# Gate tiles kept to their plan from both sides, and the first two gate tiles of a layer computed side by side

## The chip, the core and the metric

The kernel runs on one core of one Trainium2 chip. What counts is the device time of one launch in microseconds, the median of the runs. The core's engines run their own instruction streams and meet only through semaphores: TensorE (PE: matrix products and transposes; PEld is its weight load), VectorE (DVE), ScalarE (ACT), GpSimd (POOL), and SyncE (SP), which issues the transfers.

## The reference

A backbone of two layers over 512 latent tokens and 256 context tokens, width 1024, all in float32. A layer makes six modulation vectors out of a conditioning vector, modulates and normalizes its input, runs four kinds of attention over one large projection, weighs each attention's projected output with a gate, and ends with a feed-forward block.

```python
mod = (jax.nn.silu(c) @ lp['w_mod'] + lp['b_mod']).reshape(B, 1, N_MOD, D_MODEL)
h = modulate(x, mod[:, :, 0], mod[:, :, 1])            # the same for the context: mod_c, hc
aq, ak, av, bq, bkv, cq, ck, cv, dq, dk, dv, g = split_columns(h @ lp['w_in'])
oa, ob, oc, od = ...                                   # diff, MLA, grid and window attention
y = jnp.einsum('btke,ked->btkd', jnp.stack(outs, axis=2), w_branch)
gate = jax.nn.sigmoid(g.reshape(B, T, N_BRANCH, D_MODEL))
out = jnp.sum(gate * y, axis=2) @ w_out                # merge_branches
x = x + mod[:, :, 2] * mix
x = x + mod[:, :, 5] * conv_ffn(modulate(x, mod[:, :, 3], mod[:, :, 4]), lp)
```

The gates are 4 x 1024 of the columns of `w_in`: 32 tiles of 128 columns, which need the modulated input alone and are first used when the branches are merged. The modulation vectors 2 to 5 of a layer are also first used behind its attention.

## The kernel before

**Layout.** Activations lie with features on the partitions and the 768 tokens along the free axis (512 latent, 256 context), a width of 1024 as 8 feature tiles. A float32 product is made as three matmuls of split operands: `hh`,`whi`, then `hl`,`whi`, then `hh`,`wlo`. So a projection tile of 128 output columns takes 24 matmuls for each chunk of tokens. A weight tile comes in by DMA (`wraw`), ACT or DVE rounds it to `whi`, and DVE or POOL makes the rest `wlo`. Five such pairs of 128x512 can be held at a time (`WSLOTS`); a gate tile takes two of them.

**What sets the order.** The program's instructions are not emitted in the order of the code. A planner (`Clock`, with `defer` and `flush`) keeps a modelled time for each engine, and each engine's stream is sorted by planned start. What goes to PE next is chosen by `Flow` (L370 to L464) out of generators ("streams") of these kinds:

- `live`: the attention units of the layer, and `aux`: small work that belongs to them;
- `urgent`: the projections that attention is about to need;
- `gates`: the 32 gate tiles of the layer, then the merge and the feed-forward, used as filler wherever attention can't keep PE busy;
- `back`: the modulation vectors of later use.

`head` offers the first urgent or gate stream that is ready. In `run`, a stream of `urgent` is served while `debt` is positive; debt grows as attention steps are served. Otherwise the first ready step of `cand = aux + live + back` is taken, and only if none is ready the filler that `head` offers. `limit()` says how many gate tiles should still be left at this point of the attention, so that they last; `spared` keeps those back. Nothing pulls a gate tile forward that is behind this plan.

**The modulation vectors.** `diff_open` pushes vectors 2, 4, 3 and 5 of layer 0 to `back` while the attention runs: 64 steps, each with a load of 256 KB (`wm`) and two DVE instructions (`macc`, `maccc`, 128x512 each; one step in 8 is on ACT); every 8 steps end with transposes on PE (`tr<-ident,macc`, `tr<-ident,maccc`). `MPACE` is the least distance between two steps, in the planner's microseconds.

**The merge.** `open_merge` (L1538) opens the merge of the branches once nothing is in `urgent` or `gates` and the pool of the diff attention is closed, and that closes only when `back` is empty. It frees the modulated input (`hh`, `hl`) and uses the room for the attention outputs, which come back from DRAM (`oraw`, then split into `oh` and `ol`). `g_merge` multiplies them with `w_branch` (`d<-oh,whi` and so on).

**The gates.** `open_gates` (L803) makes one stream `g_gate` (L810) for each of the 32 tiles. In layer 0 it is called once the input of the layer has been loaded, in layer 1 at the end of layer 0; there the 512 latent tokens alone are computed, as the last layer leaves the context out. A tile is 24 matmuls into one PSUM bank per chunk, then a tanh on ACT (`gt`) and a store. The first tiles of a layer run while its features (`hh`, `hl` of feature tile 0, 1, ...) are still being made, one after the other.

Of the kernel before, what the change touches and what calls it, by code (L numbers as in the profile page):

```python
# [9 lines left out]
P = 128  # L10
NX, NC_, NT = 512, 256, 768
DM = 1024
KD = DM // P
# [22 lines left out]
MPACE = 5.5  # L36
# [190 lines left out]
def _body(tc, io, dump):  # L227
# [144 lines left out]
    class Flow:  # L372
# [5 lines left out]
        def __init__(self):  # L378
            self.aux, self.urgent, self.gates, self.back, self.pumps = [], [], [], [], []
            self.cur = None  # L380
            self.limit = lambda: 0

        def prefetch(self):
            for q in (self.urgent, self.gates):
                for i, s in enumerate(q):
                    if s.started:
                        continue
                    if s.slots > len(wfree):
                        break
                    if self.spared(q, i) and (any(x.started and not x.begun for x in q) or  # L390
                                              len(wfree) - s.slots < RESERVE):
                        break
                    if s.slots == 0:
                        s.started = i == 0
                        break
                    s.step()
                    s.started = True
                    break

# [30 lines left out]
        def run(self, streams, aux_too=False, drain=False):  # L430
            debt = 0.0
            live = [Stream(g) for g in streams]
            while True:
# [10 lines left out]
                if debt > 0 and f and (f is self.cur or f in self.urgent) and f.at() + MARGIN <= t0:  # L444
                    self.fill(f)
                    debt -= clock.pe - t0
                    continue
                cand = self.aux + live + self.back
# [14 lines left out]
                if self.urgent or (self.cur and debt > 0):  # L463
                    debt += PACE * (clock.pe - t0)  # L464
# [338 lines left out]
    def open_gates(l, h, ok, pl):  # L803
        gt_pool[:] = [pl]
        gd[:] = [dr.tile([P, NT], F32, f"gd{l}_{t}") for t in range(32)]
        for t in range(32):
            st = Stream(g_gate(l, t, h, ok, gd[t]), 2)
            st.later = True
            flow.gates.append(st)

    def g_gate(l, t, h, ok, dst):
# [3 lines left out]
        def evac(ps, o, n):  # L815
            g = gt_pool[0].tile([P, NX], F32, "gt", RB["gt"][l])
            nc.scalar.activation(g[:, :n], ps[:, :n], AF.Tanh, scale=0.5)
            nc.sync.dma_start(dst[:, o:o + n], g[:, :n])
# [9 lines left out]
    for l in range(2):  # L828
# [21 lines left out]
        flow.pumps[:] = []  # L850
        aux, urgent, gates = flow.aux, flow.urgent, flow.gates
# [692 lines left out]
        def open_merge():  # L1544
# [6 lines left out]
            flow.pumps.append(load_o)  # L1551
            gates.extend(Stream(g_merge(f, k), 1) for k, f in order)
# [283 lines left out]
        if not last:  # L1836
            xd = [dr.tile([P, NX], F32, f"xd{f}") for f in range(KD)]
            hok = covered(norms)
            flow.limit = lambda: 32 - NGT
# [118 lines left out]
```

## Time and profile before

| | |
|---|---|
| median of 3 runs | 3007.7 us (3001.59 to 3012.05) |
| the profiled execution | 3005.46 us, span 3003.7 us |
| busy: PE / DVE / ACT / POOL | 96% / 67% / 44% / 24% |
| granted PE clock, mean | 0.987 of full speed |
| attention of layer 0, up to its last gate matmul | 293 to 945.2 us |
| rest of it, and the first merge tiles | 945.2 to 1001.1 us |
| start of layer 1 (first gate tile) | 1761.3 us |
| last gate tile and first merge of layer 1 | 2444.2 us |

Times within the profile are microseconds from the start of the span. A matmul's row gives its start, its duration, its engine and line, the tiles it writes and reads, and in brackets the idle time of its engine ahead of it with the instruction that ended this idle time. Durations of neighbouring matmuls overlap; the distance between two starts is what a matmul takes of PE.

### The profile page before, as it was taken

Reading aid. Unit: us, or ns where it says so; the run is one execution under the profiler, and the core shown is the slowest. Engines: PE = TensorE matmul, PEld = TensorE weight load, DVE = VectorE, ACT = ScalarE, POOL = GpSimd, SP = SyncE. Lnnn points to the kernel's source line nnn. Section 1 sums busy time; section 2 is a strip of 40 time slices with the busy share of each in tenths; the row PEclk is TensorE's granted clock in tenths of the full one; section 3 lists DMA queues with packets and bytes.
Section 4 is the critical chain, followed back from the end, with each engine's and each line's share of the span. In section 5 each row is a group of like instructions: output and inputs, shape, how many; then the busy total and the mean of one; then the engine's idle time right before and its main releaser. Section 6 shows DMA issues by size and latency. Waiting matters only on the chain. (4 is left out here: it accounts for less than half of the span.)

```text
span 3003.7 us, 45158 instructions
## 1 busy us (share of the span) xinstructions
PE 2890.9 (96%) x16404; PEld 2476.5 (82%) x16404; DVE 2013.6 (67%) x4004; ACT 1314.2 (44%) x2521; POOL 711.2 (24%) x566
## 2 busy tenths in 40 slices
PE   7999999999997999999999999999999999999998
PEld 4888879888886888888888877788888887888887
DVE  5576777776877666976665475776766777765556
ACT  4465445355554224433333244654445653433333
POOL 2111221212110232322222122122322222332222
PEclk9999999999998999999999999999999999999999
DMA  5332333323223644443332143332222245433333
GB/s 209 102 106 64 116 111 101 116 73 96 96 77 123 201 149 150 129 132 120 113 124 75 55 141 109 102 87 88 92 86 80 90 134 180 148 93 100 95 92 102
DMA packets 183455, 334.58 MB, mean 111 GB/s; under 512 B 22720, under 2 KB 39360, under 8 KB 183232
## 3 DMA queue, kind: packets, MB, share of 16 engines
q1 hardware_dynamic: 183232, 331.70, 35.4%
q8 instruction: 129, 2.11, 0.3%
q14 instruction: 94, 0.77, 0.1%
HBM read 263.97 MB, written 35.65 MB: 100 GB/s over the span
## 5 line engine op out<-in xcount | busy, mean ns | idle before, releaser
L190 POOL TENSOR_TENSOR wlo<-wraw,whi 128x512 fp32r<-128x512 f32 (+1 forms) x407 | 516.2, 1270 | 1876.6 <-ACT whi L190 1230.3
L290 PE MATMUL d<-hh,whi 128*128 128x512 f32 (+1 forms) x1736 | 632.4, 364 | 15.3 <-ACT rt L190 5.4
L290 PE MATMUL d<-hl,whi 128*128 128x512 f32 (+1 forms) x1736 | 615.9, 355 | 1.4 <-DVE hl L190 1.3
L290 PE MATMUL d<-hh,wlo 128*128 128x512 f32 (+1 forms) x1736 | 615.8, 355 | 0.0
L190 ACT CAST whi<-wraw 128x512 fp32r<-128x512 f32 (+1 forms) x537 | 319.1, 597 | 481.6 <-PE d L290 244.7
L290 PEld LDWEIGHTS d<-hh,whi 128*128 128x128 f32 x1736 | 328.8, 189 | 55.0 <-ACT rt L190 6.1
L290 PEld LDWEIGHTS d<-hh,wlo 128*128 128x128 f32 x1736 | 328.2, 189 | 48.7
L290 PEld LDWEIGHTS d<-hl,whi 128*128 128x128 f32 x1736 | 329.0, 190 | 40.6 <-DVE hl L190 3.6
L190 DVE TENSOR_SCALAR_CACHE_REDUCE S<-s 128x512 f32<-128x512 f32 (+2 forms) x576 | 287.0, 515 | 103.0 <-PE s L290 100.3
L190 DVE SCALAR_TENSOR_TENSOR pl<-tr,ph 128x512 fp32r<-128x512 f32 (+2 forms) x364 | 229.5, 650 | 107.4 <-ACT ph L190 105.1
L190 ACT CAST ph<-tr 128x512 fp32r<-128x512 f32 (+2 forms) x364 | 194.8, 558 | 224.5 <-PE tr L295 208.1
L290 PE MATMUL s<-k,qs 128*128 128x256 f32 (+2 forms) x1152 | 279.8, 335 | 7.9 <-DVE qs L190 4.1
L190 ACT ACTIVATE S<-S,stat 128x768 f32<-128x768 f32 (+2 forms) x320 | 257.9, 809 | 45.4 <-DVE stat L190 44.9
L190 DVE SCALAR_TENSOR_TENSOR wlo<-wraw,whi 128x512 fp32r<-128x512 f32 x271 | 197.6, 732 | 112.7 <-ACT whi L190 105.0
L290 PEld LDWEIGHTS s<-k,qs 128*128 128x128 f32 x1152 | 193.0, 189 | 36.4 <-DVE S L190 5.5
L295 PE MATMUL tr<-ident,S 128*128 128x128 f32 x1360 | 197.8, 273 | 3.2 <-DVE S L190 1.3
L295 PEld LDWEIGHTS tr<-ident,S 128*128 128x128 f32 x1360 | 163.6, 140 | 32.6 <-DVE S L190 2.5
L290 PE MATMUL pv<-ph,V 128*128 128x256 f32 (+2 forms) x448 | 165.0, 375 | 2.1 <-ACT ph L190 2.0
L290 PE MATMUL pv<-pl,V 128*128 128x512 f32 (+2 forms) x392 | 144.2, 372 | 8.6 <-DVE pl L190 8.5
L290 PE MATMUL s<-hh,whi 128*128 128x512 f32 (+1 forms) x368 | 131.7, 358 | 0.4 <-ACT hh L190 0.4
L290 PE MATMUL s<-hl,whi 128*128 128x512 f32 (+1 forms) x368 | 131.2, 357 | 0.4 <-DVE hl L190 0.3
L290 PE MATMUL s<-hh,wlo 128*128 128x512 f32 (+1 forms) x368 | 130.7, 355 | 0.0
(277 smaller groups left out, 6047.8 us busy)
## 6 DMA issues: line engine op xcount, KB each, us to landing
wraw<-wp_d SPq DMA_DIRECT2D x220, 256.0 KB, 2.9
wraw<-wup_d SPq DMA_DIRECT2D x176, 256.0 KB, 2.6
wm<-wm_d SPq DMA_DIRECT2D x160, 256.0 KB, 2.9
wraw<-wd_d SPq DMA_DIRECT2D x74, 256.0 KB, 2.7
gd<-gt SPq DMA_DIRECT2D x64, 256.0 KB, 2.0
wraw<-wb_d SPq DMA_DIRECT2D x64, 256.0 KB, 3.5
k<-k SPq DMA_DIRECT2D x80, 192.0 KB, 3.4
wraw<-wo_d SPq DMA_DIRECT2D x56, 256.0 KB, 2.9
```

Of the source, the lines that this page charges most:

```text
L190: self.enter(op, args, kw, lambda: fn(*args, **kw))
L290: clock.defer(t, None, clock.pe - t, names, lambda: real.tensor.matmul(out, lhsT, rhs, start=start, stop=stop))
L295: clock.defer(t, None, clock.pe - t, names, lambda: real.tensor.transpose(out, src, ident[:rows, :rows]))
```

## The change

The diff has five parts. (1) `MPACE` is 7.0 in place of 5.5. (2) A flag `planned` is true from the start of a layer's attention until the merge opens; while it is true the modulation steps stand first among the candidates, ahead of `aux` and the attention, not last. (3) `due()` is true when more gate tiles are left than the plan plus one; then the gate stream is served against `debt` as an urgent one is. (4) The first two gate tiles of a layer become one stream `g_gates2` with four weight slots: for each feature tile the three matmuls of the first gate tile, then the three of the second, into two banks. (5) The limit at the end of layer 0 counts this double stream as one: 31 - (NGT - 1) = 28 as 32 - NGT before.

```diff
-MPACE = 5.5
+MPACE = 7.0
...
+            self.planned = False
...
+        def due(self):
+
+            return self.planned and len(self.gates) > self.limit() + 1
...
-                if debt > 0 and f and (f is self.cur or f in self.urgent) and f.at() + MARGIN <= t0:
+                if debt > 0 and f and (f is self.cur or f in self.urgent or self.due()) and f.at() + MARGIN <= t0:
...
-                cand = self.aux + live + self.back
+                cand = self.back + self.aux + live if self.planned else self.aux + live + self.back
...
-                if self.urgent or (self.cur and debt > 0):
+                if self.urgent or self.due() or (self.cur and debt > 0):
                     debt += PACE * (clock.pe - t0)
...
-        for t in range(32):
-            st = Stream(g_gate(l, t, h, ok, gd[t]), 2)
+        for st in [Stream(g_gates2(l, h, ok), 4)] + [Stream(g_gate(l, t, h, ok, gd[t]), 2) for t in range(2, 32)]:
             st.later = True
             flow.gates.append(st)
...
+    def g_gates2(l, h, ok):
+        ws = [load_w(io[f"wp{l}"][PJ_G + t]) for t in range(2)]
+        yield loaded(ws[0] + ws[1])
+        yield need(open=True, ok=lambda: ok(0, NX))
+        rh, rl = h()
+        for o, n in X_CHUNK if l else ALL_CHUNKS:
+            banks = []
+            for k in range(KD):
+                for i in range(2):
+                    (wh, wl), s = ws[i][k], slice(o, o + n)
+                    first = () if k else ("d",)
+                    yield need(wh, wl, rh[k][:, s], rl[k][:, s], *first, ok=lambda: ok(o, n, k), open=k + i == 0)
+                    if k == 0:
+                        banks.append(ps_tile("d"))
+                    mm(banks[i][:, :n], wh, rh[k][:, s], start=k == 0, stop=False)
+                    mm(banks[i][:, :n], wh, rl[k][:, s], start=False, stop=False)
+                    mm(banks[i][:, :n], wl, rh[k][:, s], start=False, stop=k == KD - 1)
+            for i in range(2):
+                gate_out(gd[i], banks[i], o, n, l)
...
+        flow.planned = True
...
+            flow.planned = False
             gates.extend(Stream(g_merge(f, k), 1) for k, f in order)
...
-            flow.limit = lambda: 32 - NGT
+            flow.limit = lambda: 31 - (NGT - 1)
             open_gates(1, lambda: nxt[1:], hok, late)
```

Both programs have the same instructions on PE in the same numbers; their order differs from the start to the first merge tiles of layer 0 and through the attention of layer 1, and is the same in between and behind.

**The opening of the merge in layer 0, on PE.** `oh` and `ol` are an attention output's two parts, `macc` and `maccc` the last modulation vector, `pv` the product of probabilities and values, `s` scores. Before:

```order
L290 MATMUL pv_120_192<-pl_197_506,V_179_488 128x384
L290 MATMUL pv_120_192<-ph_198_507,V_179_488 128x256
L290 MATMUL pv_120_192<-pl_199_508,V_179_488 128x256
L295 MATMUL tr_69_141<-ident_4_65,ex_209_518 128x128 x4
L295 MATMUL tr_73_145<-ident_4_65,ex_209_518 128x128 x2
L295 MATMUL tr_69_141<-ident_4_65,macc_227_2595 128x128 x4
L295 MATMUL tr_73_145<-ident_4_65,maccc_228_2596 128x128 x4
L290 MATMUL d_152_461<-oh0_301_8679,whi3_13_79 128x512
L290 MATMUL d_152_461<-ol0_302_8680,whi3_13_79 128x512
```

Now:

```order
L290 MATMUL s_45_117<-band_245_2671,ident_4_65 128x128
L290 MATMUL pv_120_192<-ph_198_507,V_179_488 128x384
L290 MATMUL pv_120_192<-pl_199_508,V_179_488 128x384
L295 MATMUL tr_73_145<-ident_4_65,S_185_494 128x128
L295 MATMUL tr_73_145<-ident_4_65,S_187_496 128x128
L290 MATMUL d_152_461<-oh0_249_8399,whi3_13_79 128x512
L290 MATMUL d_152_461<-ol0_250_8400,whi3_13_79 128x512
L290 MATMUL d_152_461<-oh0_249_8399,wlo3_14_80 128x512
L290 MATMUL d_152_461<-oh1_252_8402,whi3_13_79 128x512
L290 MATMUL d_152_461<-ol1_253_8403,whi3_13_79 128x512
L290 MATMUL d_152_461<-oh1_252_8402,wlo3_14_80 128x512
L290 MATMUL pv_120_192<-ph_196_505,V_179_488 128x384
```

The first merge tile stood behind the last transposes of the modulation vectors, and these behind the whole attention; it now stands 16 rows behind the last gate tile, with about 240 rows of attention work after it and between its matmuls, and the transposes of the modulation vectors stand some 500 rows earlier.

**The last modulation steps, on DVE in layer 0.** `ot` is an attention output, `S` scores copied out of PSUM, `pl` the low part of the probabilities, `wm` the loaded weights. Before:

```order
L190 SCALAR_TENSOR_TENSOR ot_200_509<-ot_200_509,tr_69_141 128x512
L190 SCALAR_TENSOR_TENSOR ot_200_509<-ot_200_509,tr_73_145 128x256
L190 SCALAR_TENSOR_TENSOR macc_227_2595<-wm_226_2594,csil_17_83,macc_227_2595 128x512
L190 SCALAR_TENSOR_TENSOR maccc_228_2596<-wm_226_2594,csil_17_83,maccc_228_2596 128x512
L190 SCALAR_TENSOR_TENSOR macc_227_2595<-wm_231_2599,csil_17_83,macc_227_2595 128x512
L190 SCALAR_TENSOR_TENSOR maccc_228_2596<-wm_231_2599,csil_17_83,maccc_228_2596 128x512
```

Now:

```order
L190 SCALAR_TENSOR_TENSOR macc_227_2653<-wm_226_2652,csil_17_83,macc_227_2653 128x512
L190 SCALAR_TENSOR_TENSOR maccc_228_2654<-wm_226_2652,csil_17_83,maccc_228_2654 128x512
L190 SCALAR_TENSOR_TENSOR pl_199_508<-tr_73_145,ph_198_507 128x512
L190 SCALAR_TENSOR_TENSOR pl_197_506<-tr_69_141,ph_196_505 128x256
L190 TENSOR_SCALAR S_159_468,stat_201_510<-s_46_118 128x256
L190 TENSOR_SCALAR S_163_472,stat_201_510<-s_45_117 128x256
L190 SCALAR_TENSOR_TENSOR macc_227_2653<-wm_230_2656,csil_17_83,macc_227_2653 128x512
L190 SCALAR_TENSOR_TENSOR maccc_228_2654<-wm_230_2656,csil_17_83,maccc_228_2654 128x512
L190 SCALAR_TENSOR_TENSOR pl_199_508<-tr_73_145,ph_198_507 128x384
```

The last eight of these instructions stood in one row behind all attention work of DVE; they now stand in pairs among it, ahead of `pl` and `S` that attention waits for.

**The start of layer 1, on PE.** `hh0` and `hl0` are the two parts of feature tile 0 of the modulated input, `d` the two gate tiles' banks. Before:

```order
L290 MATMUL d_154_463<-hh0_403_14595,whi0_7_73 128x512
L290 MATMUL d_154_463<-hl0_411_14603,whi0_7_73 128x512
L290 MATMUL d_154_463<-hh0_403_14595,wlo0_8_74 128x512
L290 MATMUL d_154_463<-hh1_404_14596,whi0_7_73 128x512
L290 MATMUL d_154_463<-hl1_412_14604,whi0_7_73 128x512
L290 MATMUL d_154_463<-hh1_404_14596,wlo0_8_74 128x512
```

Now:

```order
L290 MATMUL d_153_462<-hh0_403_14595,whi4_15_81 128x512
L290 MATMUL d_153_462<-hl0_411_14603,whi4_15_81 128x512
L290 MATMUL d_153_462<-hh0_403_14595,wlo4_16_82 128x512
L290 MATMUL d_152_461<-hh0_403_14595,whi3_13_79 128x512
L290 MATMUL d_152_461<-hl0_411_14603,whi3_13_79 128x512
L290 MATMUL d_152_461<-hh0_403_14595,wlo3_14_80 128x512
L290 MATMUL d_153_462<-hh1_404_14596,whi4_15_81 128x512
```

Six matmuls instead of three stand between one feature tile and the next. The sixth needs `wlo3`; POOL makes it behind two additions of `nacc` that stood ahead of the same instruction's place before as well.

## Rows read from the trace of the kernel before

**Rows 1.** The page's first part: busy time, share of span, and instructions of each engine.

```profile
PE 2890.9 (96%) x16404; PEld 2476.5 (82%) x16404; DVE 2013.6 (67%) x4004; ACT 1314.2 (44%) x2521; POOL 711.2 (24%) x566
```

**Rows 2.** Busy time by stretch, granted clock, DMA share: end of layer 0's attention.

```profile
core 0: us, PE busy (x) PEld busy (x) DVE busy (x) ACT busy (x) POOL busy (x), PEclk, DMA share, GB/s
945.24:1001.08 55.84, 38.00 (x183) 29.34 (x182) 36.41 (x58) 18.21 (x32) 6.61 (x4) 0.82 0.71 229
960.73:981.21 20.48, 10.05 (x28) 7.00 (x29) 11.82 (x16) 6.08 (x9) 4.74 (x3) 0.50 0.88 296
```

**Rows 3.** Timeline of PE there: start, duration, instruction, [idle ahead <- what ended it].

```profile
956.18 0.44 PE L295 MATMUL tr<-ident,ex 128*128 128x128 f32 x2 [0.17 <-DVE ex L190]
964.73 1.12 PE L295 MATMUL tr<-ident,macc 128*128 128x128 f32 x4 [8.12 <-DVE macc L190]
...
969.75 0.79 PE L290 MATMUL d<-oh,whi 128*128 128x512 f32 x1 [3.04 <-ACT whi L190]
...
971.95 0.63 PE L290 MATMUL d<-oh,whi 128*128 128x512 f32 x1
972.38 0.63 PE L290 MATMUL d<-ol,whi 128*128 128x512 f32 x1
...
976.23 0.80 PE L290 MATMUL d<-oh,whi 128*128 128x512 f32 x1 [2.80 <-ACT oh L190]
```

**Rows 4.** Timelines of DVE and ACT there.

```profile
962.25 0.75 DVE L190 SCALAR_TENSOR_TENSOR macc<-wm,csil,macc 128x512 f32<-128x512 f32 x1 [1.56 <-DMA wm<-wm_d]
...
966.33 0.83 ACT L190 CAST oh<-oraw 128x768 fp32r<-128x768 f32 x1 [10.14 <-DMA oraw<-od]
...
975.34 0.83 ACT L190 CAST oh<-oraw 128x768 fp32r<-128x768 f32 x1 [4.42 <-DMA oraw<-od]
```

**Rows 5.** Busy time by stretch, and timeline of PE, where layer 1 opens its merge.

```profile
2444.21:2458.20 13.99, 10.03 (x47) 7.83 (x45) 9.12 (x23) 7.91 (x18) 2.57 (x2) 0.88 0.78 246
...
2449.29 0.69 PE L290 MATMUL pv<-pl,V 128*128 128x384 f32 x1 [1.84 <-DVE pl L190]
...
2456.35 0.50 PE L290 MATMUL d<-ol,whi 128*128 128x512 f32 x1 [0.51 <-DVE ol L190]
```

**Rows 6.** Busy time by stretch, and timelines of PE and POOL, where layer 1 starts.

```profile
1761.25:1792.84 31.59, 27.23 (x102) 19.30 (x101) 21.58 (x41) 14.44 (x28) 8.38 (x7) 0.89 0.33 107
1766.27:1773.10 6.83, 5.63 (x12) 3.31 (x12) 5.96 (x9) 3.45 (x7) 1.27 (x1) 0.50 0.22 73
...
1763.52 0.49 PE L290 MATMUL d<-hh,whi 128*128 128x512 f32 x1 [0.67 <-ACT hh L190]
...
1766.51 0.80 PE L290 MATMUL d<-hh,whi 128*128 128x512 f32 x1 [1.28 <-ACT hh L190]
...
1776.03 0.48 PE L290 MATMUL d<-hh,whi 128*128 128x512 f32 x1
...
1781.68 0.39 PE L290 MATMUL d<-hh,whi 128*128 128x512 f32 x1
...
1761.71 2.19 POOL L190 TENSOR_TENSOR nacc<-nacc,nsq 128x256 f32<-128x256 f32 x2 [0.71 <-ACT nsq L190]
...
1764.72 1.46 POOL L190 TENSOR_TENSOR wlo<-wraw,whi 128x512 fp32r<-128x512 f32 x1 [0.83 <-ACT whi L190]
```

**Rows 7.** Busy time by stretch where layer 0 starts.

```profile
48.61:59.23 10.62, 10.33 (x48) 8.63 (x49) 9.26 (x18) 9.16 (x18) 1.30 (x1) 0.84 0.25 86
```

**Rows 8.** Busy time by stretch in the attention of layers 0 and 1.

```profile
293.00:945.24 652.24, 634.34 (x4039) 563.99 (x4038) 489.50 (x1161) 334.88 (x722) 142.57 (x97) 0.99 0.31 97
1792.84:2444.21 651.37, 636.61 (x3636) 546.20 (x3635) 444.43 (x1066) 336.60 (x660) 158.54 (x117) 1.00 0.30 91
```

**Rows 9.** The modulation steps in layer 0: instructions with duration ns min/median/max; loads' landing.

```profile
L190 DVE SCALAR_TENSOR_TENSOR macc<-wm,csil,macc x56: 735/747/958, 310.1 to 963.9; 128x512 f32<-128x512 f32 x56
L190 DVE SCALAR_TENSOR_TENSOR maccc<-wm,csil,maccc x56: 736/745/1773, 310.7 to 964.6; 128x512 f32<-128x512 f32 x56
...
DMA to landing us min/median/max: 2.6/2.9/5.7
```

More of the change, by code (lines that the diff above doesn't have):

```diff
@@ L805, in open_gates, with gate_out @@
         gd[:] = [dr.tile([P, NT], F32, f"gd{l}_{t}") for t in range(32)]
-        for t in range(32):
-            st = Stream(g_gate(l, t, h, ok, gd[t]), 2)
+        for st in [Stream(g_gates2(l, h, ok), 4)] + [Stream(g_gate(l, t, h, ok, gd[t]), 2) for t in range(2, 32)]:
             st.later = True
             flow.gates.append(st)
+    def gate_out(dst, ps, o, n, l):
+        g = gt_pool[0].tile([P, NX], F32, "gt", RB["gt"][l])
+        nc.scalar.activation(g[:, :n], ps[:, :n], AF.Tanh, scale=0.5)
+        nc.sync.dma_start(dst[:, o:o + n], g[:, :n])
+    def g_gates2(l, h, ok):
[17 more added lines that the diff above has]
+                gate_out(gd[i], banks[i], o, n, l)
     def g_gate(l, t, h, ok, dst):
@@ L815, in evac @@
         def evac(ps, o, n):
-            g = gt_pool[0].tile([P, NX], F32, "gt", RB["gt"][l])
-            nc.scalar.activation(g[:, :n], ps[:, :n], AF.Tanh, scale=0.5)
-            nc.sync.dma_start(dst[:, o:o + n], g[:, :n])
+            gate_out(dst, ps, o, n, l)
         yield need(open=True, ok=lambda: ok(0, NX))
```

## The prediction

> **What bounds the kernel now.** The first part of the page says PE: busy 2890.9 us of a span of 3003.7, and DVE, next, 67% [rows 1]. Both programs run the same matmuls. So the change can win nothing but the 113 us in which PE is idle, and what a halved clock adds after such an idle. The question is where these lie. I read the busy time by stretch next, and in the dearest stretch the timelines of PE, then of the engine that ends its waits.
>
> The dearest stretch is the end of layer 0's attention, 945.24 to 1001.08 [rows 2]. PE is busy 38.00 of 55.84 us, idle 17.84. The granted clock is 0.50, the lower of the two levels, from 960.73 to 981.21, which begins while PE stands idle; in that time PE works 10.05 us, which the higher level would do in half. At the lower level neighbouring 512-column matmuls start 0.43 us apart (971.95, 972.38) [rows 3], at the higher one 24 of them take 1776.03 to 1781.68, 0.235 each [rows 6]. The stretch thus loses 17.84 + 5.0 = 22.9 us. The timeline names the causes: 8.12 us for the last modulation step on DVE, 3.04 and 2.80 us for the first merge tile's weights and operands [rows 3]. On DVE the last steps stand in a row; one waits 1.56 us for its load. ACT stood idle 10.14 us before the first attention output arrived, and 4.42 before the next [rows 4]. Nothing is left on PE to cover this: attention and gates are through.
>
> Layer 1 has no modulation steps here and opens its merge under its attention: 13.99 us with PE busy 10.03, idle 3.96, clock 0.88 [rows 5]. A clock of 0.88 means 0.24 of 13.99 = 3.4 us at the lower level, worth about 1.5. It loses 5.5 us.
>
> The third stretch is the start of layer 1, 1761.25 to 1792.84: idle 31.59 - 27.23 = 4.36 us, and 5.63 us of work at the lower clock, half of which, 2.8, is lost: 7.2 us [rows 6]. Its waits come once for each feature tile (0.67, 1.28): three matmuls of 0.235 take 0.7 us and the next feature is not made yet.
>
> **The change part by part.** *A, modulation first and gates on time (parts 1 to 3 of the diff), at the end of layer 0's attention.* The order shows the modulation's last transposes some 500 PE rows earlier, the gates at their end earlier, and the merge's first matmul right behind them under the rest of the attention. The 8.12 us go. What is late next are the attention outputs: `oraw` can only be loaded when the last gate tile has released the modulated input, then ACT or DVE rounds it, DVE makes `ol`, and these now queue among `ph`, `pl` and `S`. That is the situation of layer 1, which loses 5.5. So A = 5.5 - 22.9 = -17.4 us. Bounds: if the attention covers it all, about 2 us of the loss are left, -21; if both pairs of outputs are waited for as now (3.04 + 2.80, and 5.0 at the lower clock), 11 are left and some more for attention's waits behind them, -10. I take the row of layer 1, since its order there is the nearest.
>
> *B, two gate tiles side by side at the start of layer 1 (parts 4 and 5).* Six matmuls, 1.4 us, now stand between one feature tile and the next. The first tile's 24 hold PE from 1761.25 to the start of the second at 1776.03, 1.8 us a feature where 0.7 would do [rows 6]; side by side, both tiles end a little behind the last feature, near 1776 to 1778, instead of 1781.7. But a new wait stands in it: the sixth matmul needs `wlo3` from POOL, behind two `nacc` additions (2.19 us from 1761.71) and 1.46 us of its own from 1764.72 at the earliest now [rows 6]. That puts the sixth matmul near 1765.5, some 2.8 us behind the fifth; behind it, PE catches up with features that are already there. I leave 3.5 us of the 7.2: B = -3.7. Bounds: -6 if only the wait for the norm is left, -1 if POOL's wait comes with a stretch of lower clock as long as now. Who waits for it: the rest of both tiles, and behind them the tile's tanh, which nothing needs soon.
>
> *The start of layer 0.* Here features cost no wait: 10.62 us with PE busy 10.33 [rows 7]. Side by side wins nothing; 0, between -1 and +1. The first projection comes 24 matmuls later, and as many are saved behind it.
>
> *D, attention in a new order.* In both layers gates move within the attention, and in layer 0 the modulation's 64 loads on SP's queue, 112 DVE instructions of 0.75 us and 16 on ACT move with them [rows 9]. None is added. PE is idle there 652.24 - 634.34 = 17.9 us in layer 0 and 14.8 in layer 1, DVE is busy 75% and 68% [rows 8]. The loads land in 2.9 us against 7 between two steps, so they are covered; the queue of SP carries 97 GB/s there against 229 at the end [rows 2, 8]. A pair of 1.5 us ahead of `pl` or `S` on DVE delays PE only where no gate matmuls are at hand, and keeping to the gate plan puts some at hand. I see reasons of both signs, and neither excludes the other: 0, between -10 and +9.
>
> Sum: -17.4 - 3.7 + 0 + 0 = -21 us. The profiled execution of 3005.5 us (2.2 below the median) would become 2984.4, the median 3007.7 - 21 = **2987**.
>
> *A rule that speaks against the change.* The longest modulation instruction of 112 took 1.77 us, while the medians of 0.747 and 0.745 stand next to the minima of 0.735 [rows 9], beside a POOL that is busy 142.6 of 652 us [rows 8]. So the trace shows such a block seldom. The Trainium skill, page "SBUF — State Buffer", section "SBUF: two separate sides", says that DVE and GpSimd share a pair of ports as an exclusive lock: a DVE instruction with two SBUF inputs and a GpSimd one that reads SBUF exclude each other, and the later one waits in full. `macc` and `maccc` are such instructions. By that rule each would meet POOL in 22% of cases and wait some 0.65 us, an estimate; put first in line, the whole 112 x 0.22 x 0.65 = 16 us could come through to PE, and the sum would be -5 in place of -21.
>
> **The rivals.**
> 1. *The merge's loads take the place of the modulation's wait.* The first pair of outputs is late, as now, ACT holds its queue on `oraw` while `ph` stands behind it, and attention stops with it. For: ACT's 10.14 and 4.42 us behind `oraw` [rows 4], DMA share 0.88 in that stretch [rows 2]. Against: layer 1's 0.51 us [rows 5]. A gives -8 instead of -17.4: 3007.7 - 8 - 3.7 = 2996.
> 2. *Attention gives it back.* Each modulation step, now first, delays PE by 0.3 us: 64 x 0.3 = +19: 3006, no difference. For: DVE at 75%, and `pl` is what PE waits for at 2449.29 [rows 5]. Against: the same steps stood there before, at a distance of 5.5 and not 7. The rule of the ports belongs here.
> 3. *Slower.* The same mechanism with the whole pair of 1.5 us on PE's path half of the time, as gates that are kept to plan are not at hand where the step is: 64 x 0.75 = +48, so 3007.7 - 21 + 48 = 3035. It becomes slower than 0.3% (9 us) from (21 + 9) / 64 = 0.47 us a step. Against: PE is idle 17.9 us in that whole stretch with the steps already in it [rows 8].
> 4. *Attention gains too.* Gates on time fill half of the 17.9 + 14.8 us, less what remains anyway: -10 more, 2977.
>
> That the change doesn't do what it says, with the merge behind the attention as before, the order excludes.
>
> **How the numbers follow.** A measurement of this kernel tells about 0.3%, 9 us, from no change. The forecast of 2987 has 0.51, rival 4 0.15, rival 1 0.15, rival 2 0.13, rival 3 0.06. Forecast, rival 4 and rival 1 are faster by over 0.3%, but for the upper edge of rival 1 (0.03): faster 0.78. Within 0.3%: rival 2 and that edge, 0.16. Slower: 0.06. For the range, the sum's bounds are -10 - 1 + 9 above and -21 - 6 - 10 below; these don't fall together. To the lower side I go to 2971, past rival 4, to the upper to 3003, which takes in rival 1 and stops short of rivals 2 and 3.
>
> **What would show it.** Right for A: no wait for `macc` on PE; the first `d<-oh` before attention's last `pv`; the stretch between last gate and the first merge tiles with under 6 us of idle and a window at the lower clock of less than 7 us, not 20. Right for B: in layer 1 the two tiles end 48 matmuls within some 16 us of their start, with one wait of 2 to 3 us for `wlo` from POOL. Right for D: PE's idle time between the start of the steps and the last gate stays at 17.9 +- 9 us. Wrong: waits for `pl`, `S` or `ph` behind `macc` in attention (rivals 2, 3), or for `oh`, `ol` at the opening with over 8 us (rival 1).

## The result and the profile after

The changed kernel takes 2988.64 us (median of 5 runs, 2984.45 to 2994.62); the kernel before 3007.7 (median of 5 as well). The ratio is 0.9937, with a 95% interval of 0.9923 to 0.9951: faster by 19 us, where 21 had been forecast. The profiled execution took 2988.98 us with a span of 2987.1, against 3003.7 before.

To compare stretches in which the two kernels do the work in another order, I use one measure throughout: the **loss** of a stretch is its time minus what its matmuls would take, each at the median distance between starts of its shape at the higher clock in the trace of the kernel before (0.23 us for 512 columns, 0.12 for 256). Stretches are cut at equal counts of PE instructions. Loss is idle time, what the lower clock costs, and whatever else puts two starts further apart than that median. Each figure is read from one profiled execution.

| loss, us | before | after | forecast of the difference | measured |
|---|---|---|---|---|
| start of layer 0 (two gate tiles) | 2.2 | 6.4 | 0 | +4.2 |
| attention of layer 0 | 36.2 | 32.7 | 0 (-10 to +9, both layers) | -3.5 |
| its end and the opening of the merge | 26.9 | 8.5 | -17.4 | -18.4 |
| the merge behind that | 4.0 | 10.1 | not in the sum | +6.0 |
| start of layer 1 | 8.9 | 4.1 | -3.7 | -4.8 |
| attention and merge of layer 1 | 34.3 | 34.2 | 0 | -0.1 |
| the rest, the same program | 42.9 | 43.0 | 0 | +0.1 |

The last column adds up to -16.5 us, which is by how much the two profiled executions differ (3005.46 and 2988.98 us). The medians differ by 19.

**The end of layer 0's attention.** First the same matmul counts before and after by stretch (span of the stretch, PE busy, PEld, DVE, ACT, POOL, granted clock, DMA share, GB/s); the row of before covers 20 us more than the first of [rows 2], to start at an equal count:

```profile
924.70:1001.08 76.38, 58.54 (x322) 47.67 (x321) 49.92 (x99) 29.50 (x61) 6.61 (x4) 0.87 0.56 181
```

```profile
927.89:984.88 56.99, 52.94 (x322) 46.66 (x320) 42.43 (x103) 29.87 (x68) 5.91 (x4) 0.94 0.51 169
```

Idle time of PE falls from 17.8 to 4.1 us. The timeline of PE and of ACT after, which answers to [rows 3, 4], shows the opening:

```profile
939.04 0.44 PE L290 MATMUL pv<-ph,V 128*128 128x384 f32 x1 [1.37 <-ACT ph L190]
...
940.06 0.48 PE L290 MATMUL d<-oh,whi 128*128 128x512 f32 x1
...
945.65 0.50 PE L290 MATMUL d<-oh,whi 128*128 128x512 f32 x1 [2.02 <-ACT oh L190]
946.65 0.50 PE L290 MATMUL d<-ol,whi 128*128 128x512 f32 x1 [0.50 <-DVE ol L190]
...
984.52 0.28 PE L290 MATMUL pv<-pl,V 128*128 128x256 f32 x1
...
944.77 0.83 ACT L190 CAST oh<-oraw 128x768 fp32r<-128x768 f32 x1 [4.06 <-DMA oraw<-od]
```

PE no longer waits for `macc`. The first `d<-oh` starts without idle time, 44 us ahead of attention's last `pv` (984.52). The second pair of outputs is still waited for (2.02), because ACT waits 4.06 us for its transfer. One wait of 1.37 us is attention's own, for `ph`.

**The start of layer 1**, which answers to [rows 6]:

```profile
1748.24:1774.99 26.75, 24.60 (x102) 19.44 (x101) 20.23 (x37) 13.00 (x24) 10.89 (x9) 0.94 0.37 118
...
1751.72 0.50 PE L290 MATMUL d<-hh,wlo 128*128 128x512 f32 x1 [2.15 <-POOL wlo L190]
...
1753.03 0.63 PE L290 MATMUL d<-hl,whi 128*128 128x512 f32 x1
1753.46 0.63 PE L290 MATMUL d<-hh,wlo 128*128 128x512 f32 x1
...
1747.56 2.43 POOL L190 TENSOR_TENSOR nacc<-nacc,nsq 128x256 f32<-128x256 f32 x2
1749.95 1.72 POOL L190 TENSOR_TENSOR wlo<-wraw,whi 128x512 fp32r<-128x512 f32 x1
```

The waits for each feature are gone; the one wait is the forecast one, the sixth matmul for `wlo` behind two `nacc` on POOL. Of the 4.1 us lost, 2.15 are this wait, and most of the rest is the lower level behind it: from 1753.03 on the starts lie 0.43 us apart.

**The start of layer 0**, by stretch as in [rows 7] (96 matmuls here, 48 there), PE and ACT:

```profile
49.67:72.90 23.23, 20.96 (x96) 17.30 (x97) 11.05 (x19) 10.81 (x22) 1.67 (x1) 0.85 0.18 62
...
65.58 0.39 PE L290 MATMUL d<-hh,whi 128*128 128x256 f32 x1 [2.11 <-ACT gt L190]
...
62.20 0.60 ACT L190 ACTIVATE gt<-d 128x512 f32<-128x512 f32 x1 [4.58 <-PE d L290]
64.93 0.60 ACT L190 ACTIVATE gt<-d 128x512 f32<-128x512 f32 x1 [2.13 <-DMA gd<-gt]
```

Here a wait appeared that was not forecast. In layer 0 a tile has two chunks of tokens. Both tiles end their first chunk together; the second tile's tanh waits 2.13 us until the first one's store has left the single `gt` tile, and the second tile's next chunk waits 2.11 us for the PSUM bank that this tanh empties. The stretch's clock of 0.85 contains two windows at the lower level: one at its start, as before, and a new one behind that wait.

**The merge behind it** has idle time of 1.60, 2.67 and 1.85 us where before had 1.55 and 1.82, all for `g` on DVE. The row at 1057.83 is of the kernel before, the others are of the changed one:

```profile
1008.30 0.47 PE L290 MATMUL d<-oh,whi 128*128 128x512 f32 x1 [2.67 <-DVE g L190]
...
1045.68 0.47 PE L290 MATMUL d<-oh,whi 128*128 128x512 f32 x1 [1.85 <-DVE g L190]
...
1057.83 0.47 PE L290 MATMUL d<-oh,whi 128*128 128x512 f32 x1 [1.82 <-DVE g L190]
...
1004.74 0.83 ACT L190 CAST oh<-oraw 128x768 fp32r<-128x768 f32 x1 [4.15 <-DMA oraw<-od]
...
1005.61 1.94 DVE L190 SCALAR_TENSOR_TENSOR ol<-oraw,oh 128x768 fp32r<-128x768 f32 x2 [2.53 <-ACT oh L190]
1007.47 0.68 DVE L190 SCALAR_TENSOR_TENSOR g<-g,d 128x512 f32<-128x512 f32 x1
```

The product `g`, which frees a bank of PSUM for PE, stands on DVE behind two `ol` of the next branch, and these wait for `oh`, which waits on ACT for its transfer. Of the 6.0 us, 2.8 are idle time (6.1 against 3.4 in all). The rest is the lower level, which followed the waits of 2.67 and 1.85; the second of these stood there before, with 1.82, and none followed it. So not all of the 6.0 is the change's.

**The attention of layer 0.** Over an equal count of matmuls from about 293 us on, PE is idle 14.9 us where before it was 17.9. The longest wait in it:

```profile
498.98 1.30 PE L295 MATMUL tr<-ident,S 128*128 128x128 f32 x4 [5.61 <-DVE S L190]
...
493.71 5.61 DVE L190 SCALAR_TENSOR_TENSOR S<-S,stat,S 128x768 f32<-128x768 f32 x6
```

PE waits for six `S` steps of attention itself, which DVE works off in one row; none of them is of the modulation.

### The profile page after: what moved, and what is told of

It reads as the page before. It is cut to its first block, busy times and chain, and to the rows that moved or that the text cites. A ratio compares the mean times of both kernels' runs of the same rounds, so it can differ in the third digit from the quotient of the medians.

```text
span 2987.1 us, 45145 instructions
## 1 busy us (share of the span) xinstructions
PE 2885.2 (97%) x16404; PEld 2477.5 (83%) x16404; DVE 2004.4 (67%) x4001; ACT 1316.3 (44%) x2525; POOL 704.0 (24%) x565
## 3 DMA queue, kind: packets, MB, share of 16 engines
q8 instruction: 129, 2.11, 0.3%
## 5 line engine op out<-in xcount | busy, mean ns | idle before, releaser
L290 PE MATMUL d<-hh,whi 128*128 128x512 f32 (+1 forms) x1744 | 639.3, 367 | 11.4 <-DVE qs L190 4.2
L290 PEld LDWEIGHTS d<-hl,whi 128*128 128x128 f32 x1744 | 330.9, 190 | 37.4 <-DVE hl L190 0.5
L290 PEld LDWEIGHTS s<-k,qs 128*128 128x128 f32 x1152 | 193.8, 189 | 37.4 <-DVE S L190 5.1
L290 PE MATMUL d<-oh,whi 128*128 128x512 f32 (+1 forms) x316 | 118.4, 375 | 13.3 <-DVE g L190 7.9
```

The lines of the kernel that those rows point to most:

```text
L290: clock.defer(t, None, clock.pe - t, names, lambda: real.tensor.matmul(out, lhsT, rhs, start=start, stop=stop))
```

## The experiments

Twelve kernels were run. The table gives the losses of each by the same stretches; the medians are of the runs of that kernel, the ratio is against runs of the kernel before on the same chip, with its 95% interval. The medians come from several chips, where the kernel before took 3007.7 to 3010.6 us, so the ratios compare better than the medians; the losses are those of one execution each. "Merge opens" says whether the first merge matmul of layer 0 stands under the attention in PE's order, with attention's matmuls behind it, or behind all of them.

| kernel | median us | ratio | merge opens | start L0 | attention L0 | end L0 | merge | start L1 | attention L1 |
|---|---|---|---|---|---|---|---|---|---|
| before | 3007.7 | | behind | 2.2 | 36.2 | 26.9 | 4.0 | 8.9 | 34.3 |
| after | 2988.6 | 0.9937 (0.9923, 0.9951) | under | 6.4 | 32.7 | 8.5 | 10.1 | 4.1 | 34.2 |
| e1 | 3042.9 | 1.0110 (1.0093, 1.0127) | behind | 5.8 | 45.8 | 48.3 | 2.1 | 2.5 | 36.8 |
| e2 | 3009.7 | 1.0002 (0.9990, 1.0014) | behind | 6.4 | 43.8 | 17.9 | 2.7 | 4.1 | 39.1 |
| e3 | 2990.2 | 0.9944 (0.9924, 0.9964) | under | 5.3 | 31.7 | 9.5 | 6.6 | 3.1 | 36.9 |
| e4 | 2988.4 | 0.9928 (0.9906, 0.9949) | under | 1.9 | 36.3 | 8.1 | 3.7 | 8.8 | 40.2 |
| e5 | 2985.8 | 0.9922 (0.9902, 0.9941) | under | 2.2 | 37.8 | 7.1 | 3.0 | 4.1 | 37.0 |
| e6 | 2988.9 | 0.9929 (0.9908, 0.9950) | under | 5.8 | 32.3 | 8.2 | 7.4 | 4.1 | 36.6 |
| e7 | 3020.2 | 1.0036 (1.0022, 1.0049) | behind | 6.3 | 52.3 | 26.7 | 3.7 | 2.5 | 35.7 |
| e8 | 2993.3 | 0.9954 (0.9935, 0.9972) | under | 1.9 | 33.2 | 7.2 | 6.8 | 9.1 | 39.1 |
| e9 | 3001.3 | 0.9975 (0.9961, 0.9988) | under | 3.6 | 42.2 | 7.6 | 8.9 | 2.5 | 38.5 |
| e10 | 2994.7 | 0.9960 (0.9947, 0.9973) | under | 6.2 | 51.5 | 0.1 | 3.8 | 2.8 | 30.2 |
| e11 | 2974.5 | 0.9891 (0.9878, 0.9904) | under | 2.9 | 37.4 | 7.4 | 6.9 | 2.5 | 25.7 |
| e12 | 3015.1 | 1.0022 (1.0010, 1.0034) | behind | 2.0 | 33.9 | 32.2 | 3.9 | 8.6 | 43.8 |

e6 has the changed kernel's order on PE throughout, as told below, and so shows how far a second execution differs: up to 0.6 us at the start of layer 0, 2 to 4 in longer stretches. e8 and e11 have the same order on PE up to the start of layer 1, and their losses in layer 0's attention differ by 4 us.

**e1, modulation last again.**

```diff
-                cand = self.back + self.aux + live if self.planned else self.aux + live + self.back
+                cand = self.aux + live + self.back
```

> The changed kernel with the modulation steps again last among the candidates; gates kept to plan, the slower pace and the side-by-side tiles stay. In its order the merge of layer 0 opens behind all attention work again (its first matmul right behind the last macc transposes), while the gates end early. Theory (the 18 us at the end of layer 0's attention come from opening the merge under the attention, and that needs the modulation out of the way as well as the gates): the stretch loses its 18 us again, with a wait of 5 to 9 us for macc on PE and a window of about 20 us at the lower clock; 2988.6 + 18 = 3006 us. Rival (gates on time are enough): 2990 us, no wait for macc over 2 us.

The direction is the theory's, the size is not: 3042.9 us, 54 over the changed kernel where 18 were expected. The end loses 48.3 us, 40 more than in the changed kernel, and the attention ahead of it another 13. PE there:

```profile
982.40 1.12 PE L295 MATMUL tr<-ident,macc 128*128 128x128 f32 x4 [7.80 <-DVE macc L190]
...
999.55 1.11 PE L295 MATMUL tr<-ident,macc 128*128 128x128 f32 x4 [15.18 <-DVE macc L190]
```

In this order two groups of eight modulation steps, not one, are left for the end, behind the last gate tile, and nothing covers them.

**e2, no rule for late gates.**

```diff
-            return self.planned and len(self.gates) > self.limit() + 1
+            return False
```

> The changed kernel without the rule that serves gates behind plan; modulation first, pace 7.0 and side-by-side tiles stay. In its order the gates of layer 0 reach to the end of the attention and the merge opens behind it, but the modulation is through 600 rows earlier. Theory: the wait for macc (8.1 us and its share of the lower clock) is gone, the wait for the first attention outputs is not, since nothing covers it: the stretch loses about 8 to 12 us more than in the changed kernel; 2997 to 3001 us. Rival (the modulation steps alone were the wait): 2988 to 2990 us, the stretch loses under 3 us more.

The stretch lost 9.4 us more than in the changed kernel, within the theory's 8 to 12. The wait for `macc` is gone and its place is taken, almost in full, by the wait for the first output and weight, which ACT rounds in this order, 5.43 us idle for the output's transfer:

```profile
972.42 0.79 PE L290 MATMUL d<-oh,whi 128*128 128x512 f32 x1 [7.74 <-ACT whi L190]
...
979.30 0.79 PE L290 MATMUL d<-oh,whi 128*128 128x512 f32 x1 [3.45 <-ACT oh L190]
...
969.54 1.81 ACT L190 CAST oh<-oraw 128x768 fp32r<-128x768 f32 x2 [5.43 <-DMA oraw<-od]
```

So the modulation steps alone were not the wait; being able to open under the attention is. The median, 3009.7, is 9 us above what I expected; the attention of layer 0 also lost 11 us more. e2 keeps both the pace of 7.0 and the double stream in layer 0, so by itself it doesn't tell which of them needs the rule.

**e3, the old pace.** `MPACE = 7.0` becomes 5.5.

> The changed kernel with the pace of the modulation steps at 5.5 as before. In its order the merge of layer 0 opens at the same place as in the changed kernel. Theory: the pace does nothing for the opening; 2989 us, within 5 of the changed kernel, attention's losses within 5 us. Rival (closer steps put first delay attention on DVE): the stretch from 293 to 930 us loses 8 us or more over the changed kernel, 2997 us or more.

2990.2 us, attention of layer 0 at 31.7 instead of 32.7: the theory. With the rule in place the pace does nothing that can be measured.

**e4 and e5, the double stream: in neither layer, in layer 1 alone.**

```diff
-        for st in [Stream(g_gates2(l, h, ok), 4)] + [Stream(g_gate(l, t, h, ok, gd[t]), 2) for t in range(2, 32)]:
+        for st in [Stream(g_gate(l, t, h, ok, gd[t]), 2) for t in range(32)]:
...
+        for st in ([Stream(g_gates2(l, h, ok), 4)] if l else []) + [Stream(g_gate(l, t, h, ok, gd[t]), 2) for t in range(2 * l, 32)]:
```

> The changed kernel with the first two gate tiles one after the other, as before, in both layers; all else stays. Theory (side by side gains some 4.8 us at the start of layer 1 and loses some 4 to 5 us at the start of layer 0, where the second tile's tanh waits for the first one's store): layer 1's start loses 4 to 5 us more than in the changed kernel, layer 0's start 4 us less, 2988 us, within 4 of it. Rival (layer 0's start differs by chance, as its stretches of lower clock do from run to run): only the loss in layer 1 returns, 2993 us.

> The changed kernel with the double gate stream in layer 1 only; layer 0's first two tiles one after the other. Theory (the pair costs 4 to 5 us at the start of layer 0): the start of layer 0 is as before (no wait for gt there, second chunk without idle), the start of layer 1 as in the changed kernel; 2984 us, 4 less than the changed kernel. Rival (that start differs by chance): 2988 us.

e4 also takes back part 5 of the diff. The start of layer 1 loses 8.8 us without the double stream and 4.1 with it. The start of layer 0 loses 1.9 to 2.9 in the five kernels without it there (e4, e5, e8, e11, e12), 2.2 before, and 5.3 to 6.4 in the seven with it (after, e1, e2, e3, e6, e7, e10); so this is no chance. e4 comes out at 2988.4, as forecast from the two. e5, at 2985.8, gains 3 of the 4 us that it should; the intervals are too wide to tell it from the changed kernel, and 5 us more of loss in its attention stand against the 4 at the start and 7 in the merge.

**e6, two gt tiles.** The count of buffers of `gt` was made 2 until the layer's attention begins.

> The changed kernel with two gt tiles instead of one as long as layer 0's attention has not begun (and at the end of layer 0); the order on PE is the same up to the start. Theory (the second tile's tanh waits for the first one's store because there is one gt tile, and holds the PSUM bank that the second chunk needs): the wait of 2.1 us on PE at 65.6 us goes to under 0.7 us, and the window at the lower clock behind it; 2985 us. Rival (both banks are full at the same time and one tanh of 0.6 us behind the other is the wait, whatever the tiles): the wait stays over 1.2 us; 2988 us.

The edit missed its place. By the code, the first tanh of layer 0 is emitted when the attention's pool, with its one `gt` tile, is already the current one. The order on PE is the changed kernel's, the wait was still 2.10 us, and so was the time, 2988.9 us. It says nothing about the cause.

**e9, the second tanh into another tile.**

```diff
-    def gate_out(dst, ps, o, n, l):
-        g = gt_pool[0].tile([P, NX], F32, "gt", RB["gt"][l])
+    def gate_out(dst, ps, o, n, l, tag="gt"):
+        g = gt_pool[0].tile([P, NX], F32, tag, RB[tag][l])
...
-                gate_out(gd[i], banks[i], o, n, l)
+                gate_out(gd[i], banks[i], o, n, l, "gt" if l or not i else "sw")
```

> The changed kernel, but the second tile of layer 0's double stream gets its tanh into the tile sw, which lies idle then, and not into the one gt tile; the order on PE is the same. Theory (the second tanh waits for the first one's store because both use one tile, and holds the PSUM bank of the next chunk): the wait of 2.1 us on PE near 65 us falls under 0.8 us, the start of layer 0 (96 matmuls) loses 2 to 3 us and not 6; 2985 us. Rival (the two banks being full at once is the wait): over 1.2 us stay; 2988 us.

ACT now runs the two one behind the other:

```profile
63.11 0.60 ACT L190 ACTIVATE gt<-d 128x512 f32<-128x512 f32 x1 [5.37 <-PE d L290]
63.81 0.60 ACT L190 ACTIVATE sw<-d 128x512 f32<-128x512 f32 x1
```

PE's wait fell from 2.11 to 0.07 us and the loss of the start from 6.4 to 3.6: the cause of the wait is the one tile and its store. Most of what is left over the 2.2 of before is a longer time at the lower level at the start of the stretch, 5.2 us against 3.4. But the kernel became slower, 3001.3. My expectation was wrong in saying that PE's order is the same: it is for the first thousand rows of PE or so, and behind them the planner put the attention in another order. That order loses 42.2 us in layer 0's attention where the changed kernel loses 32.7. One of its waits, with DVE ahead of it:

```profile
675.60 0.69 PE L295 MATMUL tr<-ident,ex 128*128 128x128 f32 x2 [5.00 <-DVE pl L190]
...
672.15 0.75 DVE L190 SCALAR_TENSOR_TENSOR macc<-wm,csil,macc 128x512 f32<-128x512 f32 x1
672.82 0.75 DVE L190 SCALAR_TENSOR_TENSOR maccc<-wm,csil,maccc 128x512 f32<-128x512 f32 x1
674.11 0.75 DVE L190 SCALAR_TENSOR_TENSOR macc<-wm,csil,macc 128x512 f32<-128x512 f32 x1 [0.54 <-DMA wm<-wm_d]
...
674.91 1.22 DVE L190 SCALAR_TENSOR_TENSOR pl<-tr,ph 128x512 fp32r<-128x512 f32 x2
```

Three modulation instructions stand here ahead of the `pl` that PE waits for, and the third waits for its load as well. That is the mechanism of rivals 2 and 3, with the modulation *first* among the candidates.

**e7, the double stream alone.** The kernel before with `g_gates2` and nothing else.

> The kernel before with the side-by-side tiles alone (no change of pace, modulation last, no rule for late gates). Theory: minus 4.8 us at the start of layer 1, plus 4 to 5 at the start of layer 0, and the merge of layer 0 opens behind the attention as before: 3007 us, no difference that can be measured. Rival (the forecast's price of B holds for the whole): 3003 us.

Both theories fell: 3020.2, slower than before by 0.2 to 0.5%. The two starts are as in the theory (6.3 and 2.5). What came on top lies in layer 0's attention, 52.3 us, of which 26 in a stretch of 1000 matmuls (548.7 to 725.9) where before lost 2.6. Two waits of over 5 us stand in it; PE and DVE:

```profile
557.29 1.30 PE L295 MATMUL tr<-ident,S 128*128 128x128 f32 x4 [5.34 <-DVE S L190]
...
552.03 5.60 DVE L190 SCALAR_TENSOR_TENSOR S<-S,stat,S 128x768 f32<-128x768 f32 x6
...
651.89 0.69 PE L295 MATMUL tr<-ident,nsq 128*128 128x128 f32 x2 [5.48 <-DVE pl L190]
...
649.16 0.75 DVE L190 SCALAR_TENSOR_TENSOR maccc<-wm,csil,maccc 128x512 f32<-128x512 f32 x1
649.83 0.75 DVE L190 SCALAR_TENSOR_TENSOR macc<-wm,csil,macc 128x512 f32<-128x512 f32 x1
650.49 0.75 DVE L190 SCALAR_TENSOR_TENSOR maccc<-wm,csil,maccc 128x512 f32<-128x512 f32 x1
651.15 0.69 DVE L190 SCALAR_TENSOR_TENSOR pl<-tr,ph 128x512 fp32r<-128x512 f32 x1
```

The first is the wait for six `S` steps that the changed kernel has too; the modulation has no part in it. Ahead of the second, three modulation instructions, 2.0 of the 5.48 us, stand right ahead of the `pl` that the row of PE names, with no gate tile on PE beside them. That much is rival 3's mechanism, here with the modulation *last* among the candidates. It is a small part of the 26 us. Why the steps gather in these places, and why this order loses so much, no run isolates.

**e8, modulation first alone.** The kernel before with the change's line for the candidates (the one that e1 undoes) and `planned`, and nothing else.

> The kernel before with the modulation steps first among the candidates as the only change. In its order the merge of layer 0 opens under the attention, some 25 rows later than in the changed kernel, although late gates are not pulled forward. Theory: the opening under the attention is what counts, whichever part brings it: about 17 of the 18 us are gained; 3007.7 - 17 = 2990 us, wait for macc gone. Rival (first in line without the slower pace and the gate rule, the steps delay attention): 3000 us or more, with losses of 8 us or more over the kernel before between 293 and 930 us.

2993.3 us, 3 over the theory's figure: the end of layer 0 loses 7.2 instead of 26.9. PE there, busy time and the opening:

```profile
922.74:978.36 55.62, 51.62 (x323) 44.83 (x321) 42.80 (x98) 31.45 (x70) 11.13 (x7) 0.97 0.54 173
...
936.82 0.48 PE L290 MATMUL d<-oh,whi 128*128 128x512 f32 x1
```

One line, with the flag that it reads, brings the whole of A. Its attention loses 33.2, not more than before.

**e12, the rule for late gates alone.** The kernel before with `due()`.

> The kernel before with the rule that serves gates behind plan as its only change. In its order the gates of layer 0 end 140 rows earlier and the merge stays behind the attention and the last modulation steps. Theory (gates on time without the modulation on time take away the cover at the end): the end of the attention loses more than the 27 us of before, with waits for macc; 3015 us or more. Rival (gates on time gain by themselves): 3000 us or less.

3015.1, slower than before by 0.1 to 0.3%, as the theory has it. The end loses 32.2 us, 5 more than before, with a wait of 5.97 us for `macc` and one of 2.51 in an attention that has no gate tile left:

```profile
950.22 1.39 PE L295 MATMUL tr<-ident,S 128*128 128x128 f32 x4 [2.51 <-ACT S L190]
...
967.35 1.12 PE L295 MATMUL tr<-ident,macc 128*128 128x128 f32 x4 [5.97 <-DVE macc L190]
```

Another 9.5 us were lost in layer 1's attention, where the rule changes the order too.

**e10, each modulation instruction twice.**

```diff
                             stt(a, w, sc_, a, ALU.mult, ALU.add)
+                            if pace == MPACE and wd == 512:
+                                stt(a, a, 1.0, a, ALU.mult, ALU.max)
```

> The changed kernel with a second DVE instruction of the same size behind each of the 112 macc and maccc instructions of layer 0's attention (the maximum of the tile with itself, the result is the same): 112 x 0.75 = 84 us of DVE work more at the disputed place. Theory (a modulation step that stands first and is spread out is covered by gate matmuls): PE pays under 0.3 us a step, under 17 us; 2989 to 3005 us. Rival 3's price (half of the added work comes through to PE): 42 us; 3030 us.

84 us of DVE work more cost 6 us of the median. Its merge opens earlier, within the attention stretch, so attention and end are read together: 51.6 us against 41.2, 10.4 us for the 56 steps on DVE, 0.19 a step, where the 6 us of the median are 0.11. Rival 3's price of 0.75 is out. The planner counts the added work and places the gates for it, so this is the price with planning.

**e11, what was left of the change.** Modulation first, and the double stream in layer 1; pace 5.5, no `due()`, layer 0's tiles one after the other.

> The kernel before with two things only: modulation steps first among the candidates, and the double gate stream in layer 1. Pace 5.5, no rule for late gates, layer 0's gate tiles one after the other. The merge of layer 0 opens under the attention in its order. Theory (these two carry the whole gain, the rule for late gates and the pace only repair what the double stream does to layer 0's plan): 2993.3 - 4.8 = 2988 us. Rival (rule and pace have a gain of their own): 2995 us or more.

2974.5 us, ratio 0.9891: 14 us better than the changed kernel, the fastest of all, and 13.5 below what the theory said. 3.5 us of it are the start of layer 0. The largest part, 8.5 us, is layer 1's attention, 25.7 instead of 34.2. Why that order is better was not settled: e8, also without the rule for late gates, loses 39.1 there, e7 35.7, and their orders differ. It is a property of this one plan until another run shows more.

## Why the prediction was right

**A, the end of layer 0's attention: right in size, too wide in cause.** -18.4 measured, -17.4 forecast, and the rows that were to show it are there: no wait for `macc`, `d<-oh` before the last `pv`, idle of 4.1 us and two windows of 3.4 at the lower clock. Taking layer 1's opening [rows 5] as the price was the step that held. But the prediction gave the credit to three parts together, and added that gates kept to plan put cover at hand. Modulation first does it alone (e8); the rule for gates alone loses (e12); the pace does nothing with the rule in place (e3). Where the double stream in layer 0 and the pace of 7.0 come together, the rule is needed (e2): there the gates reach to the end of the attention and the merge can't open earlier. Neither of the two seems to need it alone. In the order of e2 built with the pace of 5.5 the merge opens under the attention, and so it does in that of e11 built with 7.0; these two orders were not timed. So the rule repairs, in layer 0, what other parts of the change do to the plan.

**B, the start of layer 1: right.** -4.8 against -3.7; the new wait for `wlo` was forecast at 2.8 us and measured 2.15. e4 and e5 switch the gain off and on. Its size hangs on whether the lower level follows that wait: the start loses 4.0 to 4.1 where it does, and 2.5 to 3.1 where it does not, which is a gain of up to 6.4.

**The start of layer 0: the failed step.** Forecast 0 with bounds of 1, measured +4.2. The prediction looked at the features alone [rows 7], and said of B's tanh that nothing needs it soon. That holds in layer 1 with its one chunk. In layer 0 the same tanh frees the bank of the second chunk, and two that end together meet the one `gt` tile. e9 shows it for the wait, which is half of the 4.2; in this execution the lower level behind it is most of the other half. The store's time was to be had before: gd<-gt lands in 2.0 us by the page.

**The merge: a missing term.** +6.0 in this execution, 2.8 of it idle time; +3.3 in e6, the same order again. The kernels whose merge opens at about the same place lose 6.6 to 10.1 there, those that open some 50 rows earlier (e4, e5) 3.0 to 3.7. The prediction asked what is late next at the opening, but not at the following branches, whose outputs come by the same transfers.

**D, attention: right within its bounds.** -3.5 and -0.1 against 0 between -10 and +9; the idle time that was to stay at 17.9 within 9 is 14.9. That this range was needed is seen in the experiments: changes that leave the same work lose between 31.7 and 52.3 us there.

So the total was right, 2988.6 against 2987. In the profiled executions two things that were not foreseen, +4.2 and +6.0, stand against three small gains of 1.0, 1.1 and 3.5 beyond the forecast: -16.5 us, not -21. That the medians differ by 19, and come within 2 us of the forecast, is in part luck.

**The rivals.** Rival 1, the loads in the place of the modulation, is what e2 shows, but not what the change did. Rivals 2 and 3 did not come in the changed kernel, whose longest wait in attention is not for the modulation, and e10 puts the price of a step far under rival 3's. Their mechanism exists all the same: e9 has it with modulation first, e7 with modulation last. Rival 4 asked for 10 us from the attention; the 3.6 of both layers are no more than two executions of one order differ by.

## What to carry to other kernels

Work that others will need and that is put last among the candidates can be left for where there is no cover, at the end; put it first, spread out, and the end can be opened under other work. That does not keep it from standing ahead of a late step (e9), so look for that in the order that comes out. Switch off each part of a change of several parts, since here one line and half of another gave more than the whole. Where two streams are made to end together, ask for every buffer that their ends share, chunk by chunk.

## What the runs showed of the hardware

The modulation instructions have two tiles of SBUF as inputs. In the trace after, of the 112 on DVE 24 overlap in time with an instruction on POOL, and the nine that took over 1 us are all among them; none of the other 88 took so long. Before it was 9 overlaps and two. Here are the longest, and one that was not delayed, on DVE, each with POOL beside it:

```profile
717.65 1.82 DVE L190 SCALAR_TENSOR_TENSOR maccc<-wm,csil,maccc 128x512 f32<-128x512 f32 x1
...
717.63 1.30 POOL L190 TENSOR_TENSOR wlo<-wraw,whi 128x512 fp32r<-128x512 f32 x1 [1.11 <-DVE whi L190]
...
714.61 0.74 DVE L190 SCALAR_TENSOR_TENSOR maccc<-wm,csil,maccc 128x512 f32<-128x512 f32 x1
...
714.69 1.82 POOL L190 TENSOR_TENSOR wlo<-wraw,whi 128x512 fp32r<-128x512 f32 x1 [7.00 <-ACT whi L190]
```

In the first pair DVE starts 0.02 us after POOL, and ends 0.54 us after POOL ended. In the second DVE starts first: it takes its usual 0.74 us, and POOL ends 1.16 us after it. The whole trace has it so. In the 12 overlaps with a 512-column instruction of POOL that started first and still ran 0.2 us or more, DVE ended about 0.55 us after POOL; where DVE started first it lost nothing. Two overlaps with 12-column instructions of POOL cost DVE nothing. The Trainium skill, page "SBUF — State Buffer", section "SBUF: two separate sides", describes this as an exclusive lock of a shared pair of ports, and the trace agrees. The price of it here is small: the 112 instructions took 91.0 us in all after, 85.7 before. The prediction's share of 22% was met, with 24 of 112 (before it was 9), but not its 16 us: over 112 times 0.75 the delays on DVE are 7 us, and layer 0's attention as a whole lost 3.5 us less than before.

How long PE was idle does not tell alone whether its clock falls to the lower of the two levels. The wait for `wlo` at the start of layer 1 is 2.15 us, within 0.01, in each of the ten kernels with the double stream there. In four of them (after, e2, e5, e6) a stretch at 0.50 follows it, as the starts 0.43 us apart from 1753.03 on show, and in the other six none. In layer 0's merge after, the waits of 2.67 and 1.85 us were each followed by such a stretch, the one of 1.60 was not; before, those of 1.55 and 1.82 were not.
